# A decoder trunk on one core: feed-forward tiles in pairs, full-array compressed values, a second row by halves, another attention order

## The chip, the cores and the metric

The kernel runs on one core of a Trainium2 chip. TensorE (PE in the profile) multiplies: LDWEIGHTS brings a stationary operand of up to 128 x 128 into the array (PEld), MATMUL streams a moving operand of up to 512 columns past it and adds into PSUM. VectorE (DVE), ScalarE (ACT) and GpSimd (POOL) work element by element; ScalarE evaluates functions from a table, which ACT_TABLE_LOAD brings in. SyncE (SP) issues the DMAs. Each engine works through its own queue in order and waits for others by semaphores. The metric is the time of one execution on the device in microseconds; lower is better.

## The reference, cut to what matters

Two decoder layers over 256 tokens of 1024 values, in float32. Each has a half-step feed-forward in front and behind; the first layer mixes by a gated convolution, the second by sparse attention, whose keys and values are made once, from the state between the layers.

```python
def swiglu_ffn(x, w_in, w_out):
    gate, up = jnp.split(x @ w_in, 2, axis=-1)
    return (jax.nn.silu(gate) * up) @ w_out
...
v_c = compress(kv[:, :, 0, 1], pe_v, w1_v, w2_v)      # gelu(blocks @ w1) @ w2
...
for i in range(DEPTH):
    h = h + 0.5 * swiglu_ffn(rmsnorm(h, ffn1_norm[i]), ffn1_w_in[i], ffn1_w_out[i])
    hn = rmsnorm(h, mix_norm[i])
    h = h + (short_conv_mixer(hn, ...) if i < N_A_LAYERS else nsa_mixer(hn, ..., kv))
    h = h + 0.5 * swiglu_ffn(rmsnorm(h, ffn2_norm[i]), ffn2_w_in[i], ffn2_w_out[i])
```

A feed-forward goes from 1024 to 2 x 2816 and back. In attention each query takes three softmaxes: over 15 compressed blocks, over selected blocks and over a window. The queries are normalised per head (a reciprocal square root), and gates (sigmoid) weigh the three.

## The kernel before, in words

**Products by halves.** Every float32 operand is cut into a high part (rounded to the format that TensorE takes at full rate, "fp32r") and a low part (the rest). A weight unit of 128 x 1024 thus becomes two tiles: "wh", cast by ScalarE (line 165, Stream.high), and "wl", the difference, by VectorE (line 182, Stream.low). An activation tile "xs" or "act" holds 256 high and 256 low columns side by side. A product is then a *wide* one, wh against all 512 columns (line 353), and a *narrow* one, wl against the 256 high columns (line 358), summed in PSUM; the wide product's two halves are added when PSUM is read.

**Weights.** One stream W carries all weights in the order of their use. DMAs bring 1 MB pieces into three staging tiles "ws". pump casts units ahead: at most NBUF = 6 units (three column tiles) beyond those freed; take hands units out, done frees them. A `weave` interleaves one pump with each step of an evacuation and, if asked to (rest), fills up to the limit at its end.

**Feed-forward.** ffn_in runs over NF = 22 column tiles of 128 gates and 128 ups. For each, a_group does two columns: 16 wide products (2 columns x 8 rows of 128), then 16 narrow ones, into one of two PSUM buffers "mm". Then `total` reads the buffer (ScalarE line 367, VectorE line 368), ffn_evac multiplies by the row norm (372), applies SiLU (ScalarE 384, VectorE 385) and cuts the result into halves (361, 362). A callback bg does other work behind given tiles. There are four feed-forwards. The first begins in first_tiles, where three column tiles are computed row by row as x and the weights arrive; their sums wait, and while they are worked off, one more every third tile, only two units are pumped per tile. out_proj (lines 467 and 469) does the way back: per output column 22 wide and 22 narrow products.

**First rows.** In first_tiles row 0 is done by halves: first the 256 high columns of x, then the low ones. For each later row both halves of x, then the weights of columns 0 and 1, are cut in turn: `highs` on ScalarE (line 510), `lows` on VectorE (507); then the products (513).

**Shared keys and values.** In the third feed-forward bg does the compression: c_hidden of the values behind tile 14 (W1AT), c_total and its GELU behind tile 15 (gelu: GpSimd 820 to 825 with a ScalarE tanh at 823), kc_norm with a square root behind 16 (841, 843), c_values behind 17 (855, 858), which multiplies in four half-array blocks.

**Attention.** The stage is an order written out by hand: ORDER is a list of words, each an operation with its indices, issued in that order to the engines' queues. The words that matter here: GT, GC, GA, GX, GE, GD gates; qs, qr, root, recip, qn queries of the first half (squares, sums, square root at line 938, reciprocal, scaling at 960); exp the preloading of the table "natural_log_exp_and_others" (line 1192); QT, QC the transposition of queries and its copy (971, 975); F one step of the projection of the second half's queries (988 to 990); SQ, RD, NW, QM their squares, sums, a reciprocal root from a logarithm and an exponential (948, 949) and scaling; S scores, M minima, E exponentials (1060), R, N normalisation (N on GpSimd, with the ending _d on VectorE); T, H transpositions; C, CH, CPC copies out of PSUM (on ScalarE, with _d on VectorE); V, U products with values; CP transposition of the compressed weights; WA, WD a unit's high and low part; WO pieces of the output projection. The PSUM buffers "a" are four; two are held by the second half's queries until QM_1.

Of the kernel before, what the change touches and what calls it, by code (L numbers as in the profile page):

```python
# [16 lines left out]
P = 128  # L17
# [32 lines left out]


ORDER = """
GT qs_0 F qs_1 qr_0 F F qr_1 GC root WA_0 exp recip qn_0 F qn_1 QT_0 QC_0 GA GX F GE S_0 GD WA_1 M_0_1 QT_1 M_0_0
E_0_1 F F F E_0_0 R_0_1 F WD_0 SQ_0 R_0_0 N_0_1 S_1 RD_0 QC_1 M_1_0 M_1_1 F F F E_1_0 F CM_0 N_0_0 E_1_1 S_2 F F CX_0
R_1_0 N_1_0_d CE_0 R_1_1 F T_0_1 M_2_1 E_2_1 SQ_1 CR_0 C_0_1 N_1_1 T_1_0 M_2_0 RD_1 CG_0 C_1_0 CI_0 T_0_0 NW H_0 R_2_1
C_0_0 S_3 QM_0 CL_0 QM_1 M_3_1 T_1_1 E_2_0 CP_0 M_3_0 CH_0 CPC_0 QT_2 QC_2 C_1_1 N_2_1 E_3_0 H_1 QT_3 R_2_0 T_2_1
CH_1_d S_4 QC_3 E_3_1 CM_1 N_2_0 V_0 C_2_1_d R_3_0 M_4_0 M_4_1 T_2_0 CX_1 U_0 U_1 H_2 N_3_0 O_0 P_0 R_3_1 CE_1 CR_1
C_2_0_d N_3_1 E_4_1 S_5 CG_1 V_1 T_3_1 CH_2 M_5_1 E_4_0 R_4_1 T_3_0 M_5_0 H_3 CH_3_d CI_1 CM_2 S_6 C_3_1_d N_4_1 E_5_1
O_1 T_4_1 CL_1 R_4_0 C_3_0_d R_5_1 CP_1 P_1 M_6_1 WA_2 CX_2 CE_2 CR_2 CPC_1_d V_3 E_6_1 V_2 C_4_1 N_4_0 T_4_0 M_6_0
C_4_0_d U_3 H_4 CG_2 E_5_0 CI_2 E_6_0 CH_4_d N_5_1 R_5_0 N_5_0_d U_2 S_7 CL_2 O_2 CP_2 CPC_2 V_4 O_3 U_4 O_4 WA_3  # L60
R_6_1 M_7_0 T_5_0 P_3 R_6_0 WA_4 P_2 N_6_1 P_4 E_7_0 WD_1 M_7_1 CM_3 T_5_1 N_6_0 WD_2 H_5 WO_0_a T_6_1 WO_1_a C_6_1
CX_3 R_7_0 WD_3 CE_3 T_6_0 N_7_0 C_5_0_d CH_5 E_7_1 CR_3 CG_3 CI_3 C_5_1 WO_2_a WO_3_a C_6_0_d R_7_1 T_7_0 N_7_1_d
T_7_1 U_5 C_7_0 C_7_1_d CL_3 CP_3 CPC_3 H_7 WD_4 H_6 WA_5 CH_6_d U_6 CH_7_d V_5 V_6 O_5 O_6 P_5 P_6 V_7 U_7 WD_5 O_7
WO_1_b WO_0_b P_7 WO_0_c WO_3_b WO_1_c WO_2_b WO_3_c WO_2_c
"""


# [1 line left out]
def trunk(ctx, tc, A, out):  # L69
# [132 lines left out]
                self.pump()  # L202

    W = Stream()
    W1AT = (11, 14)
    W.add(A["ffn1_w_in"][0])
    W.add(A["ffn1_w_out"][0])
    W.add(A["conv_w_in"])
# [193 lines left out]
    def ffn_in(xs, norm, R=None, bg=None, pre=None, sums=()):  # L402

        hid, sums = [], list(sums)
        box = [R]
        n0 = len(sums)

        def mid():
            if pre is not None:
                pre()  # L410
            box[0] = norm.rows()

        for f in range(n0, NF):
            o = bank2()
            a_group([o[:, 0], o[:, 1]], xs, mid if f == n0 and R is None else None, not n0)
            sums.append(total(o, 2))
            late = len(sums) > 1
            weave(ffn_evac(sums.pop(0), box[0], hid), not late)
            if late and (f - n0) % 3 == 2:
                list(ffn_evac(sums.pop(0), box[0], hid))  # L420
            if bg is not None:
                bg(f)
        return hid

    def out_evac(o, c, factor, norm, short=False):
# [72 lines left out]
    def first_tiles():  # L498

        o = [bank2(), bank2()]  # L500
        oo, o = o, [[x[:, u] for u in range(2)] for x in o] + [[bank(), bank()]]
        w = [[mk([P, 2, 4, P], t, NBUF, F32R) for t in ("wh", "wl")] for _ in range(6)]

        def lows(f, src, g):
            wh, wl = w[2 * f + g[0] // 4]
            ks = slice(g[0] % 4, g[-1] % 4 + 1)
            ve.tensor_tensor(out=wl[:, :, ks], in0=src, in1=wh[:, :, ks].bitcast(F32), op=ALU.subtract)  # L507

        def highs(f, src, g, copy=ac.copy):
            copy(w[2 * f + g[0] // 4][0][:, :, g[0] % 4:g[-1] % 4 + 1], src)  # L510

        def product(f, k, u, x, c=slice(0, 512)):
            pe.matmul(o[f][u][:, c], w[2 * f + k // 4][x][:, u, k % 4], xs[k][:, c], start=k == x == c.start == 0, stop=(k == 7 and x == 1))

        def products(f, g):
            for x in range(2):
                for u in range(2):
                    for k in g:
                        product(f, k, u, x, slice(0, (2 - x) * T))

        def third(ks):
            g = range(*ks)
            src = w2st[:, ks[0] * 2 * P:ks[1] * 2 * P].rearrange("p (k u m) -> p u k m", u=2, m=P)
            highs(2, src, g)
            lows(2, src, g)

        def more(k):
            t = sq[0].rearrange("p a t -> p (a t)")
            po.tensor_tensor(out=t, in0=t, in1=sq[k].rearrange("p a t -> p (a t)"), op=ALU.add)

        nm.high(0)
        highs(0, parts[0, (0,)], (0,), ve.tensor_copy)
        highs(1, parts[1, (0,)], (0,))
        nm.low(0)
        for f in range(2):
            lows(f, parts[f, (0,)], (0,))
        for c in (slice(0, T), slice(T, 512)):
            for f in range(2):
                for u in range(2):
                    product(f, 0, u, 0, c)  # L540
        for f in range(2):
            for u in range(2):
                product(f, 0, u, 1, slice(0, T))
        third(THIRD[1])
        square(0)
        products(2, (0,))
        for n, g in enumerate(GROUPS):
            if n == 0:
                continue
            for k in g:  # L550
                nm.tile(k, False)
            for f in range(2):
                highs(f, parts[f, g], g)
                lows(f, parts[f, g], g)
            for k in g:
                square(k)
            for f in range(2):
                products(f, g)
            if n in (2, 4):
                third(THIRD[n + 1])  # L560
            if n < 5:
                products(2, g)
            if g[-1] % 2 and g[-1] > 1:
                more(g[-1] // 2)
        po.tensor_tensor(out=nm.sq, in0=sq[0][:, 0], in1=sq[0][:, 1], op=ALU.add)
        W.units += [None] * 6
        W.take(6)
        W.done(6, False)
        W.high()
        sums = [total(x, 2) for x in oo]  # L570
        products(2, GROUPS[-1])
        W.pump(1)
        r = t2([P, 2, T])
        for u in range(2):
            ac.copy(r[:, u], o[2][u][:, T:])
        for u in range(2):
            ve.tensor_tensor(out=r[:, u], in0=o[2][u][:, :T], in1=r[:, u], op=ALU.add)
        sums.append(r)
        W.pump(1)
        q = act()  # L580
        split(nm.sq, q)
        W.pump(2)
        return sums, q
# [266 lines left out]
    def c_values(a):  # L850

        pc = bank([P, 2, 64])
        t = t1([P, 2, 64])
        a4 = t1([P, 4, 4, 16])
        po.tensor_copy(out=a4, in_=a.rearrange("p (g n) -> p g n", g=4)[:, :, None, :].to_broadcast([P, 4, 4, 16]))
        for g in range(4):
            z = slice(g % 2 * 64, g % 2 * 64 + 64)
            pe.matmul(pc[z, g // 2], a4[:, g].rearrange("p x n -> p (x n)"), w2[1], start=True, stop=True)
        for g2 in range(2):
            hi, lo = slice(g2 * 64, g2 * 64 + 32), slice(g2 * 64 + 32, g2 * 64 + 64)  # L860
            ac.copy(vc[hi, :, g2], pc[hi])
            ac.copy(t[lo].bitcast(F32R), pc[lo])
            ve.tensor_tensor(out=vc[lo, :, g2], in0=pc[lo], in1=t[lo], op=ALU.subtract)

    def bg(f):
# [3 lines left out]
        elif f == 1:  # L869
            r = inv_rms(kv["s"])  # L870
            for tt in range(2):
                v = kns[tt].rearrange("p (n d) -> p n d", d=64)
                po.tensor_tensor(out=v, in0=v, in1=r[:, tt * 8:tt * 8 + 8, None].to_broadcast([P, 8, 64]), op=ALU.mult)
        elif f in (2, 3, 4, 5):
            c_trans((f - 2) % 2, (f - 2) // 2)
        elif f in (6, 7):
            k_trans(f - 6)
        elif f == 8:
            po.tensor_tensor(out=both, in0=ident[:, :64], in1=ident[:, 64:], op=ALU.add)
            po.tensor_tensor(out=both48, in0=ident[:96, :48], in1=ident[:96, 48:96], op=ALU.add)  # L880
        elif f == 9:
            kv["rk"] = rh_split(0)
        elif f == W1AT[0]:
            kv["ak"] = c_hidden(kv["rk"])
        elif f == 12:
            kv["ak"] = c_total(kv["ak"])
            kv["rv"] = rh_split(1)
            W.limit = NBUF
        elif f == W1AT[1]:
            kv["av"] = c_hidden(kv["rv"])  # L890
            kv["kc"] = kc_second(kv["ak"])
        elif f == 15:
            kv["av"] = c_total(kv["av"])
        elif f == 16:
            kc_norm(*kv["kc"])
        elif f == 17:
            c_values(kv["av"])

# [426 lines left out]
```

## Time and profile before

| | us |
|---|---|
| median of three runs (968.42 to 969.76) | 969.49 |
| the profiled execution, whole | 967.74 |
| its span, from the first to the last instruction | 965.8 |
| TensorE busy in the span | 960.5 |
| VectorE, ScalarE, GpSimd busy | 733.4, 571.2, 133.6 |

The granted clock of TensorE is 1.00 throughout the span. The stages on TensorE: first rows and first feed-forward to 129, its way back to 190, convolution to 279, second feed-forward with its way back to 464, keys and values to 497, third feed-forward with its way back to 690, query projection and attention to 767, output projection to 778, fourth feed-forward to the end.

In a list of instructions a row gives start, duration, engine, line, operation, written and read tile, shapes and count of merged neighbours; TensorE's durations overlap, since matmuls are pipelined, so its pace is read from starts. In the chain's rows the pieces follow one another without overlap. In a table of stretches each engine has its busy time and number of instructions; the columns after are the granted clock, the DMAs' share and GB/s. In a list of waits stand the waiting instruction, what it waited for, the sum, how often, and the longest.

### The profile page before, as it was taken

How to read it: one execution, taken by the hardware profiler on the slowest of the kernel's cores; microseconds unless marked ns; L12 is line 12 of the kernel's file. 1: busy time of each engine (PE TensorE's matmuls, PEld its weight loads, DVE VectorE, ACT ScalarE, POOL GpSimd, SP SyncE). 2: the span in 40 equal slices, each digit the busy share in tenths (PEclk: the TensorE clock that was granted, in tenths of full speed). 3: DMA queues.
4: the chain of work that ended last, by engine and by line, in shares of the span. 5: the costliest groups of instructions: out<-in, count | busy, mean ns of one | idle time of the engine just before them, and what ended most of it. 6: DMA issues, size and time to landing. Idle time of an engine off the chain costs nothing.

```text
span 965.8 us, 14561 instructions
## 1 busy us (share of the span) xinstructions
PE 960.5 (99%) x5614; PEld 841.4 (87%) x5614; DVE 733.4 (76%) x1152; ACT 571.2 (59%) x972; POOL 133.6 (14%) x217
## 2 busy tenths in 40 slices
PE   9999999999999999999999999999999999999998
PEld 8888888888888888888888888888877888888888
DVE  7888876578898787766549988866579898878652
ACT  7666654455566665645556676754589676566530
POOL 2000000144520000000111013000138320000000
PEclk9999999999999999999999999999999999999999
DMA  8656655545546875555535566555510356555550
GB/s 307 211 182 218 210 183 182 201 165 204 182 172 225 234 234 175 194 198 181 211 131 175 175 223 248 183 178 191 205 46 2 131 196 238 177 184 207 181 191 22
DMA packets 28433, 177.61 MB, mean 184 GB/s; under 512 B 3099, under 2 KB 6555, under 8 KB 7756
## 3 DMA queue, kind: packets, MB, share of 16 engines
q1 hardware_dynamic: 28364, 176.69, 53.6%
q8 instruction: 44, 0.72, 0.3%
q14 instruction: 25, 0.20, 0.1%
HBM read 175.59 MB, written 1.08 MB: 183 GB/s over the span
## 4 chain that ended last, share of the span: by engine, by line
PE 98%; DVE 1%; ACT 1%; DMA 0%; issue 0%; SPq 0%
PE mm L353 36%; PE mm L358 19%; PE a L467 17%; PE a L469 9%; PE a L353 3%; PE a L358 2%; PE mm L1041 1%; PE a L692 1%; PE a L694 1%; PE a L693 1%; PE a L1118 1%; PE a L1086 1%; DMA base<-in_first_dram 0%; DVE wl L507 0%; PE a L988 0%; PE a L801 0%
## 5 line engine op out<-in xcount | busy, mean ns | idle before, releaser
L182 DVE TENSOR_TENSOR wl<-ws,wh 128x1024 fp32r<-128x1024 f32 x318 | 392.3, 1248 | 97.5 <-PE a L469 63.0
L353 PE MATMUL mm<-xs,wh 128*128 128x512 f32 x1488 | 357.4, 392 | 0.0
L165 ACT CAST wh<-ws 128x1024 fp32r<-128x1024 f32 x318 | 328.2, 1046 | 38.5 <-PE a L467 20.5
L353 PEld LDWEIGHTS mm<-xs,wh 128*128 128x128 f32 x1488 | 273.1, 188 | 52.7
L358 PEld LDWEIGHTS mm<-xs,wl 128*128 128x128 f32 x1488 | 191.6, 191 | 7.8
L358 PE MATMUL mm<-xs,wl 128*128 128x256 f32 x1488 | 194.0, 283 | 0.0
L467 PE MATMUL a<-act,wh 128*128 128x512 f32 x714 | 169.1, 390 | 0.0
L467 PEld LDWEIGHTS a<-act,wh 128*128 128x128 f32 x714 | 131.8, 188 | 26.1
L368 DVE TENSOR_TENSOR t<-mm,t 128x512 f32<-128x512 f32 x95 | 65.4, 688 | 66.1 <-ACT t L367 65.3
L367 ACT COPY t<-mm 128x512 f32<-128x512 f32 x95 | 55.6, 585 | 89.6 <-PE mm L358 84.8
L469 PEld LDWEIGHTS a<-act,wl 128*128 128x128 f32 x714 | 90.6, 191 | 2.7
L469 PE MATMUL a<-act,wl 128*128 128x256 f32 x714 | 91.8, 283 | 0.0
L314 POOL TENSOR_TENSOR sq<-sq,t 128x256 f32<-128x256 f32 x35 | 27.7, 792 | 398.0 <-ACT t L312 397.9
L384 ACT ACTIVATE t<-t 128x256 f32<-128x256 f32 x88 | 36.9, 420 | 65.5 <-DVE t L372 65.4
L297 ACT ACTIVATE xs<-base 128x256 fp32r<-128x256 f32 x48 | 24.1, 505 | 77.6 <-DVE base L427 70.2
L372 DVE TENSOR_TENSOR t<-t,R 128x512 f32<-128x512 f32 x88 | 61.6, 700 | 2.6
L361 ACT CAST act<-t 128x256 fp32r<-128x256 f32 x96 | 39.0, 406 | 29.6 <-DVE t L621 19.4
L362 DVE TENSOR_TENSOR act<-t,act 128x256 fp32r<-128x256 f32 x96 | 41.0, 427 | 5.2 <-ACT act L361 5.2
L385 DVE TENSOR_TENSOR t<-t,t 128x256 f32<-128x256 f32 x88 | 36.9, 419 | 3.6 <-ACT t L384 3.5
L427 DVE SCALAR_TENSOR_TENSOR base<-a,base 128x256 f32<-128x256 f32 x78 | 32.8, 421 | 8.1 <-PE a L469 6.1
L301 DVE SCALAR_TENSOR_TENSOR xs<-base,xs 128x256 fp32r<-128x256 f32 x48 | 25.3, 529 | 11.0 <-ACT xs L297 10.9
L1060 ACT ACTIVATE pr<-pr,sm 128x128 f32<-128x128 f32 (+1 forms) x64 | 28.3, 448 | 1.9 <-DVE sm L1049 1.9
(261 smaller groups left out, 786.2 us busy)
## 6 DMA issues: line engine op xcount, KB each, us to landing
ws<-in_ffn_w_in_dram SPq DMA_DIRECT2D x85, 1024.0 KB, 4.9
ws<-in_ffn_w_out_dram SPq DMA_DIRECT2D x44, 1024.0 KB, 4.8
ws<-in_conv_w_in_dram SPq DMA_DIRECT2D x12, 1024.0 KB, 4.8
ws<-in_w_kv_dram SPq DMA_DIRECT2D x6, 1024.0 KB, 4.8
ws<-in_conv_w_out_dram SPq DMA_DIRECT2D x4, 1024.0 KB, 4.9
ws<-in_attn_w_q_dram SPq DMA_DIRECT2D x4, 1024.0 KB, 4.9
ws<-in_attn_w_o_dram SPq DMA_DIRECT2D x4, 1024.0 KB, 4.9
base<-row_d SPq DMA_DIRECT2D x8, 256.0 KB, 6.0
```

The source lines that it names most:

```text
L165: ac.copy(h, src)
L182: ve.tensor_tensor(out=l, in0=src, in1=h.bitcast(F32), op=ALU.subtract)
L353: pe.matmul(o, u[0][:, k * P:(k + 1) * P], xs[k], start=(k == 0), stop=False)
L358: pe.matmul(o[:, :T], u[1][:, k * P:(k + 1) * P], xs[k][:, :T], start=False, stop=(k == last))
L361: ac.copy(dst[:, :T], src)
L362: ve.tensor_tensor(out=dst[:, T:], in0=src, in1=dst[:, :T].bitcast(F32), op=ALU.subtract)
L367: ac.copy(r, o[:, :, T:])
L368: ve.tensor_tensor(out=r, in0=o[:, :, :T], in1=r, op=ALU.add)
L372: ve.tensor_tensor(out=r, in0=r, in1=R[:, None, :].to_broadcast([P, n, T]), op=ALU.mult)
L384: ac.activation(s, r[:, 0], AF.Silu)
L467: pe.matmul(o, run[k][0], lhs[k], start=(k == 0), stop=False)
L469: pe.matmul(o[:, :T], run[k][1], lhs[k][:, :T], start=False, stop=(k == n - 1))
```

## The change

Five edits. (1) ffn_in takes tiles in pairs: 16 wide products of the first tile, the second tile's two wide products of row 0, the first tile's 16 narrow, its evacuation and background work, the second tile's 16 narrow, its other 14 wide, its evacuation. The next pair's wide products follow directly. A tile with the norm's sum inside, and an odd last one, stay as they were. (2) c_hidden of the values moves from tile 14 to tile 15, with its weights in the stream, and c_total from 15 to 16, behind kc_norm. (3) c_values multiplies in two full-array products. (4) Row 1 in first_tiles is done by halves like row 0, with one weight cast on VectorE, and the third tile's products between. (5) ORDER is another permutation of the steps. In it C_3_0, C_3_1, CH_3, C_5_0, C_6_0, CH_6, CH_7 lose their _d, CPC_2 gains one, and N changes engine in six places.

```diff
 ORDER = """
-GT qs_0 F qs_1 qr_0 F F qr_1 GC root WA_0 exp recip qn_0 F qn_1 QT_0 QC_0 GA GX F GE S_0 GD WA_1 M_0_1 QT_1 M_0_0
-E_0_1 F F F E_0_0 R_0_1 F WD_0 SQ_0 R_0_0 N_0_1 S_1 RD_0 QC_1 M_1_0 M_1_1 F F F E_1_0 F CM_0 N_0_0 E_1_1 S_2 F F CX_0
-R_1_0 N_1_0_d CE_0 R_1_1 F T_0_1 M_2_1 E_2_1 SQ_1 CR_0 C_0_1 N_1_1 T_1_0 M_2_0 RD_1 CG_0 C_1_0 CI_0 T_0_0 NW H_0 R_2_1
-C_0_0 S_3 QM_0 CL_0 QM_1 M_3_1 T_1_1 E_2_0 CP_0 M_3_0 CH_0 CPC_0 QT_2 QC_2 C_1_1 N_2_1 E_3_0 H_1 QT_3 R_2_0 T_2_1
...
+qs_0 GT qr_0 qs_1 exp GC F qr_1 F root F F WA_0 recip qn_0 qn_1 QT_0 GA GX QC_0 F S_0 WA_1 WD_0 M_0_1 GE QT_1 M_0_0
+E_0_1 E_0_0 QC_1 F F R_0_1 F S_1 F F F GD M_1_1 M_1_0 N_0_1 R_0_0 F S_2 CM_0 F F F F E_1_1 R_1_1 CX_0 N_0_0_d SQ_0
+N_1_1 E_1_0 R_1_0 M_2_1 CE_0 N_1_0 T_0_1 T_0_0 E_2_1 SQ_1 C_0_1 C_0_0 RD_0 CR_0 M_2_0 RD_1 CG_0 CI_0 NW T_1_0 R_2_1
+QM_0 H_0 CH_0 S_3 E_2_0 QM_1 T_1_1 CL_0 M_3_0 M_3_1 QT_2 H_1 C_1_0 N_2_1 C_1_1 CP_0 CM_1 QC_2 T_2_1 CPC_0 R_2_0 E_3_1
...
-    W1AT = (11, 14)
+    W1AT = (11, 15)
...
-        for f in range(n0, NF):
-            o = bank2()
-            a_group([o[:, 0], o[:, 1]], xs, mid if f == n0 and R is None else None, not n0)
+        def finish(f, o):
             sums.append(total(o, 2))
             late = len(sums) > 1
             weave(ffn_evac(sums.pop(0), box[0], hid), not late)
...
+        def wide(o, us, ks, last=8):
+            for x in range(2):
+                for k in ks:
+                    pe.matmul(o[:, x], us[x][0][:, k * P:(k + 1) * P], xs[k], start=(k == 0), stop=(k == last))
+
+        def narrow(o, us, last=8):
+            for x in range(2):
+                for k in range(8):
+                    pe.matmul(o[:, x, :T], us[x][1][:, k * P:(k + 1) * P], xs[k][:, :T], start=False, stop=(k == last))
+
+        f = n0
+        while f < NF:
+            o = bank2()
+            if f == n0 and R is None or f + 1 == NF:
+                a_group([o[:, 0], o[:, 1]], xs, mid if f == n0 and R is None else None, not n0)
+                finish(f, o)
+                f += 1
+                continue
+
+            u = W.take(2)
+            wide(o, u, range(8))
+            o2, u2 = bank2(), W.take(2)
+            wide(o2, u2, [0])
+            narrow(o, u, 7)
+            W.done(2, False)
+            finish(f, o)
+            narrow(o2, u2)
+            wide(o2, u2, range(1, 8), 7)
+            W.done(2, False)
+            finish(f + 1, o2)
+            f += 2
...
+        def by_halves(k, mid):
+            nm.high(k)
+            highs(0, parts[0, (k,)], (k,), ve.tensor_copy)
+            highs(1, parts[1, (k,)], (k,))
+            nm.low(k)
+            for f in range(2):
+                lows(f, parts[f, (k,)], (k,))
+            for c in (slice(0, T), slice(T, 512)):
+                for f in range(2):
+                    for u in range(2):
+                        product(f, k, u, 0, c)
+            mid()
...
+        by_halves(0, lambda: None)
         third(THIRD[1])
         square(0)
         products(2, (0,))
+        by_halves(1, lambda: products(2, (1,)))
+        square(1)
...
-        for g in range(4):
-            z = slice(g % 2 * 64, g % 2 * 64 + 64)
-            pe.matmul(pc[z, g // 2], a4[:, g].rearrange("p x n -> p (x n)"), w2[1], start=True, stop=True)
+        for q in range(2):
+            pe.matmul(pc[:, q], a4[:, 2 * q:2 * q + 2].rearrange("p g x n -> p (g x n)"), w2[1], start=True, stop=True)
...
-        elif f == 15:
-            kv["av"] = c_total(kv["av"])
         elif f == 16:
             kc_norm(*kv["kc"])
+            kv["av"] = c_total(kv["av"])
```

More of the change, by code (lines that the diff above doesn't have):

```diff
@@ L52 @@
 ORDER = """
-GT qs_0 F qs_1 qr_0 F F qr_1 GC root WA_0 exp recip qn_0 F qn_1 QT_0 QC_0 GA GX F GE S_0 GD WA_1 M_0_1 QT_1 M_0_0
-E_0_1 F F F E_0_0 R_0_1 F WD_0 SQ_0 R_0_0 N_0_1 S_1 RD_0 QC_1 M_1_0 M_1_1 F F F E_1_0 F CM_0 N_0_0 E_1_1 S_2 F F CX_0
-R_1_0 N_1_0_d CE_0 R_1_1 F T_0_1 M_2_1 E_2_1 SQ_1 CR_0 C_0_1 N_1_1 T_1_0 M_2_0 RD_1 CG_0 C_1_0 CI_0 T_0_0 NW H_0 R_2_1
-C_0_0 S_3 QM_0 CL_0 QM_1 M_3_1 T_1_1 E_2_0 CP_0 M_3_0 CH_0 CPC_0 QT_2 QC_2 C_1_1 N_2_1 E_3_0 H_1 QT_3 R_2_0 T_2_1
-CH_1_d S_4 QC_3 E_3_1 CM_1 N_2_0 V_0 C_2_1_d R_3_0 M_4_0 M_4_1 T_2_0 CX_1 U_0 U_1 H_2 N_3_0 O_0 P_0 R_3_1 CE_1 CR_1
@@ L58 @@
[L58 to L62, printed above, removed]
@@ L63 @@
-T_7_1 U_5 C_7_0 C_7_1_d CL_3 CP_3 CPC_3 H_7 WD_4 H_6 WA_5 CH_6_d U_6 CH_7_d V_5 V_6 O_5 O_6 P_5 P_6 V_7 U_7 WD_5 O_7
-WO_1_b WO_0_b P_7 WO_0_c WO_3_b WO_1_c WO_2_b WO_3_c WO_2_c
+qs_0 GT qr_0 qs_1 exp GC F qr_1 F root F F WA_0 recip qn_0 qn_1 QT_0 GA GX QC_0 F S_0 WA_1 WD_0 M_0_1 GE QT_1 M_0_0
+E_0_1 E_0_0 QC_1 F F R_0_1 F S_1 F F F GD M_1_1 M_1_0 N_0_1 R_0_0 F S_2 CM_0 F F F F E_1_1 R_1_1 CX_0 N_0_0_d SQ_0
+N_1_1 E_1_0 R_1_0 M_2_1 CE_0 N_1_0 T_0_1 T_0_0 E_2_1 SQ_1 C_0_1 C_0_0 RD_0 CR_0 M_2_0 RD_1 CG_0 CI_0 NW T_1_0 R_2_1
@@ new lines @@
+QM_0 H_0 CH_0 S_3 E_2_0 QM_1 T_1_1 CL_0 M_3_0 M_3_1 QT_2 H_1 C_1_0 N_2_1 C_1_1 CP_0 CM_1 QC_2 T_2_1 CPC_0 R_2_0 E_3_1
+QT_3 N_2_0 S_4 CH_1_d QC_3 C_2_1_d R_3_1 V_0 T_2_0 CX_1 E_3_0 H_2 M_4_0 U_0 CE_1 E_4_0 M_4_1 CH_2 C_2_0_d R_3_0 U_1
+O_0 N_3_1 E_4_1 CR_1 S_5 CG_1 V_1 CI_1 M_5_0 M_5_1 O_1 R_4_0 R_4_1 V_2 S_6 T_3_1 N_3_0 CM_2 P_0 T_3_0 E_5_1 P_1 CL_1
+CX_2 CE_2 N_4_1_d H_3 C_3_1 C_3_0 CR_2 CH_3 R_5_1 N_4_0 T_4_1 C_4_1 CG_2 CP_1 M_6_1 CI_2 CPC_1_d CL_2 T_4_0 E_5_0 V_3
+C_4_0_d H_4 U_2 M_6_0 O_2 U_3 CH_4_d R_5_0 WD_1 E_6_0 CP_2 O_3 CPC_2_d N_5_1 S_7 R_6_0 E_6_1 N_5_0 V_4 U_4 P_3 P_2
@@ L65 @@
+N_6_0 O_4 M_7_0 T_5_1 E_7_0 T_5_0 P_4 M_7_1 WA_2 H_5 R_6_1 CM_3 WO_0_a N_6_1_d WD_2 CX_3 T_6_0 C_5_1 CH_5 CE_3 WO_1_a
+E_7_1 T_6_1 CR_3 H_6 CG_3 C_6_1 R_7_0 CI_3 N_7_0_d C_6_0 CL_3 WO_2_a CP_3 U_5 CH_6 R_7_1 C_5_0 N_7_1_d CPC_3 T_7_0
+C_7_0 T_7_1 WA_3 H_7 WD_3 U_6 V_5 WA_4 CH_7 O_5 V_6 C_7_1_d V_7 O_6 U_7 P_6 P_5 WO_0_b O_7 WD_4 WO_2_b P_7 WO_0_c
+WO_1_b WO_3_a WO_1_c WO_3_b WA_5 WD_5 WO_3_c WO_2_c
 """
@@ L529, in more @@
             po.tensor_tensor(out=t, in0=t, in1=sq[k].rearrange("p a t -> p (a t)"), op=ALU.add)
[L531 to L537, printed above, removed]
+        def by_halves(k, mid):
[10 more added lines that the diff above has]
+            mid()
             for f in range(2):
                 for u in range(2):
[L540 to L543, printed above, removed]
+                    product(f, k, u, 1, slice(0, T))
+        by_halves(0, lambda: None)
         third(THIRD[1])
@@ L546, in first_tiles @@
         products(2, (0,))
+        by_halves(1, lambda: products(2, (1,)))
+        square(1)
         for n, g in enumerate(GROUPS):
-            if n == 0:
+            if n < 2:
                 continue
```

## The prediction

> **What bounds the kernel now.** I read the page first, then TensorE's waits, then the chain that ended last.
>
> ```profile
> PE 960.5 (99%) x5614; PEld 841.4 (87%) x5614; DVE 733.4 (76%) x1152; ACT 571.2 (59%) x972; POOL 133.6 (14%) x217
> ```
>
> ```profile
> PE mm L513 <- ACT wh L510: 0.8, 1, 0.8
> PE a L1086 <- ACT xs L1096: 0.4, 1, 0.4
> ```
>
> ```profile
> 28.91 3.65 PE mm L353 x16
> 32.57 1.91 PE mm L358 x16
> ...
> 117.98 3.65 PE mm L353 x16
> ...
> 144.45 5.01 PE a L467 x22
> 149.46 2.63 PE a L469 x22
> ```
>
> TensorE is busy for 99% of the span and past its warm-up waits twice, for 0.8 and 0.4 us. So the kernel gets faster only by shorter TensorE work, and every wait put into TensorE's queue is paid in full. The third fence shows what there is to shorten. A column tile is 16 wide and 16 narrow products, and from 28.91 to 117.98 lie 16 tiles: 5.567 us each. A column of an output projection, 22 and 22, takes 5.01 + 2.63 = 7.64. The six further pairs cost 2.07 us, 0.346 a pair; 16 pairs are 5.54, which leaves about 0.02 us a tile for the turn from narrow to wide and back. That is all that touching can save.
>
> **The change part by part.** *Pairs.* Numbering a phase's tiles from 0, the first feed-forward has pairs (4,5) to (20,21), the second and fourth (1,2) to (19,20), the third (0,1) to (20,21): 9 + 10 + 10 + 11 = 40, each one turn fewer. In seven pairs of the third the background's own products stand between the groups, so I count 33: 33 x 0.02 = **-0.6** (0 to -0.8).
>
> Against that stand three terms. In a pair the second tile starts its k = 0 wide products right behind the first tile's 16 wide ones, 3.65 us after the pair's start, where before it began 5.57 after; its second column at 3.88. By then its high weights must be cast, and the PSUM buffer of the tile before the pair (there are two) must be read out.
>
> ```profile
> 28.75 0.63 PE L353 MATMUL mm<-xs,wh 128*128 128x512 f32 x2
> ```
>
> ```profile
> 32.12 1.03 ACT L165 CAST wh<-ws 128x1024 fp32r<-128x1024 f32 x1
> ```
>
> ```profile
> 62.15 0.40 PE L353 MATMUL mm<-xs,wh 128*128 128x512 f32 x1
> ```
>
> ```profile
> 65.81 1.04 ACT L165 CAST wh<-ws 128x1024 fp32r<-128x1024 f32 x1
> ```
>
> *High weights, first feed-forward.* Up to tile 11, while three early sums are worked off, only two weight units are made per tile (weave without its rest), so a tile's weights come one tile ahead. Tile 4 starts at 28.75. Tile 5's second cast ends at 33.15, 4.40 after, and is wanted at 3.88: with 0.06 for the signal a wait of 0.6. Tile 10 starts at 62.15; tile 11's second cast ends at 66.85, 4.70 after, late because the extra evacuation after tile 8 fills VectorE. In a pair tile 9 ends 5.1 us behind tile 8, not 5.57, so add 0.5: wanted at 3.88, there at 5.2, a wait of 1.3. The pairs between have nothing extra ahead of them. Sum **+1.9** (1.0 to 2.0). What is late behind it is nothing: later casts run three tiles ahead.
>
> ```profile
> 784.24 3.80 PE L353 MATMUL mm<-xs,wh 128*128 128x512 f32 x16
> ```
>
> ```profile
> 788.55 0.62 DVE L368 TENSOR_TENSOR t<-mm,t 128x512 f32<-128x512 f32 x1
> ```
>
> ```profile
> 532.52 3.90 PE L353 MATMUL mm<-xs,wh 128*128 128x512 f32 x16
> ```
>
> ```profile
> 536.26 0.69 DVE L368 TENSOR_TENSOR t<-mm,t 128x512 f32<-128x512 f32 x1
> ```
>
> ```profile
> 285.94 3.35 PE L353 MATMUL mm<-xs,wh 128*128 128x512 f32 x14
> ```
>
> ```profile
> 289.15 0.62 DVE L368 TENSOR_TENSOR t<-mm,t 128x512 f32<-128x512 f32 x1
> ```
>
> *Buffers.* In the fourth feed-forward tile 1 starts at 784.24, tile 2 wants tile 0's buffer at 787.89, and VectorE, which had weight conversions and the reciprocal in front, has read it at 789.17: 1.3. In the third, tile 6 starts at 532.52 behind transpositions (0.1 more until it is wanted: 536.26), and tile 5's buffer is read at 536.95: 0.7. In the second, wanted at 289.59, read at 289.77: 0.2. Sum **+2.2** (0.5 to 2.4; the fourth's lag hangs on how the attention stage hands over).
>
> ```profile
> 593.70 0.56 PE L812 MATMUL a<-both,t 128*128 128x64 f32 x4
> ```
>
> ```profile
> 598.63 0.40 ACT L361 CAST act<-t 128x256 fp32r<-128x256 f32 x1
> 598.93 0.20 ACT L814 COPY t<-a 128x64 f32<-128x64 f32 x1
> ```
>
> ```profile
> 602.02 0.40 POOL L855 COPY t<-t 128x256 f32<-128x256 f32 x1
> ```
>
> ```profile
> 605.07 1.28 ACT L843 ACT_TABLE_LOAD   x1
> 606.37 0.31 ACT L843 ACTIVATE t<-a,epst 128x64 f32<-128x64 f32 x1
> ```
>
> ```profile
> 605.62 0.45 PE L858 MATMUL a<-small,t 128*64 128x64 f32 x8
> ```
>
> *Compressed values.* Two full-array products for four half-array ones: the group at 605.62 costs 0.39 us to the next product and a turn of some 0.1; the four full instructions at 593.70 take 0.37, so **-0.1** (0 to -0.2). What moves is dearer. Before, c_total stands behind tile 15 (593.70). ScalarE gets to its copy only after the tile's own evacuation, at 598.93; GELU and the spreading copy end at 602.42, and c_values at 605.62 finds them done. In the changed kernel c_total stands behind tile 16's narrow products, after kc_norm, and c_values behind tile 17. Since 16 and 17 are a pair, only tile 17's narrow products (1.91), 14 wide ones (3.2) and 0.5 for the two small groups lie between: 5.6 us. The chain is longer. ScalarE's queue for the tile lasts to 599.03, 5.3 after the tile's end, some of it a backlog; I take 4.6 (4.0 to 5.3). Then kc_norm's table load and square root, 1.6, now in front of the copy; then 3.5 from copy to spread values. 9.7 against 5.6: **+4.1** (3.5 to 4.8). Behind the blocked matmul all of TensorE waits.
>
> *Second row by halves.*
>
> ```profile
> 7.08 0.69 ACT L510 CAST wh<-base 128x256 fp32r<-128x256 f32 x2
> ```
>
> Row 1's first products wait for the first of two ScalarE casts (the 0.8 above, to 7.83). One cast goes to VectorE, idle there, and the first half needs no low part of x, so TensorE can start at about 7.3. The row was 0.55 late, and its gain is bounded by that; later rows hang on ScalarE and VectorE, from which one cast of 0.3 is gone: **-0.3** (0 to -0.55).
>
> *Attention order.* The same 258 steps. On TensorE I find the same products and about two fewer turns into score or half-column blocks: nothing to speak of. But "exp", the preloading of the exponential table, now stands before "root", the stage's square root.
>
> ```profile
> 703.41 0.22 ACT L938 ACTIVATE sm<-sm 128x18 f32<-128x18 f32 x1
> ```
>
> ```profile
> 703.96 1.29 DVE L960 TENSOR_TENSOR t<-mm,sm 128x512 f32<-128x512 f32 x2
> ```
>
> ```profile
> 705.58 0.60 PE L971 MATMUL a<-small,t 128*128 128x128 f32 x4
> ```
>
> ```profile
> 722.39 0.24 ACT L948 ACTIVATE sm<-sm 128x16 f32<-128x16 f32 x1
> ```
>
> ```profile
> 725.36 0.60 PE L971 MATMUL a<-small,t 128*128 128x128 f32 x4
> ```
>
> ```profile
> 701.00:706.00 5.00, 5.00 (x25) 3.94 (x24) 3.43 (x8) 3.84 (x6) 0.22 (x1) 1.00 0.63 210
> 706.00:712.00 6.00, 6.00 (x37) 4.47 (x35) 4.26 (x23) 4.84 (x17) 0.40 (x1) 1.00 0.02 4
> 712.00:718.00 6.00, 6.00 (x38) 4.31 (x36) 5.29 (x28) 5.62 (x23) 5.07 (x11) 1.00 0.01 1
> 718.00:724.00 6.00, 5.62 (x39) 4.44 (x37) 5.08 (x30) 5.35 (x20) 3.38 (x10) 1.00 0.01 1
> 724.00:730.00 6.00, 5.97 (x50) 4.35 (x50) 5.68 (x32) 6.00 (x22) 4.39 (x11) 1.00 0.00 0
> ```
>
> After the preload the square root needs its own table again (as at L843, 1.28 each), and the next exponential another. If that one is the plain exponential table, the logarithm of "NW" and the exponential behind it need one each as well: four loads more, 5.1 us of ScalarE. First place: preload and load sit between qs_1 and root, where ScalarE has at most 1.16 idle (5.00 - 3.84); I let them fill 0.75 of it, so root comes 1.8 late; the normalised queries, done at 705.25 before, come at 707.1, and QT_0, at 705.58 before, waits 1.5. Second: NW's logarithm, at 722.39 before, comes about 1.5 late (idle slices of ScalarE absorb part of the load before the gates) and brings two loads; QT_2, 725.36 before, hangs on it through VectorE and comes 4.0 late, with CP_0 (0.4), which stood before it, still to do. From 724 on ScalarE is busy 6.00 of 6.00 and TensorE 5.97, so the lag stays: **+4.4**. Ends: 1.8, if all 3.35 us idle up to 724 swallow loads; 6.5, if none does and the copies that lose their "_d" (to ScalarE, net six) add to it.
>
> The Trainium skill, page "ScalarE: Activation LUTs", section "Table sets: the hidden batching unit", states that exponential then square root means two loads since they are in different sets, and that logarithm and exponential share one named set, which speaks against this order. It prices a switch at about 2.66 us with a drain. By 2.66 the four would be 10.6 and the time some 5.5 us longer; the row at 605.07 shows the square root 1.30 after the load's start, no drain. On the sets the trace agrees: NW's logarithm and exponential run without a load between them.
>
> **The sum**: -0.6 - 0.1 - 0.3 + 1.9 + 2.2 + 4.1 + 4.4 = **+11.6 us**. The profiled execution took 967.74, so 979.3; the median of the three runs is 1.75 above it, and I predict by the median: 969.49 + 11.6 = **981.1**.
>
> **The rivals.**
> - *Loads not repeated*: the compiler keeps a table that serves, or the preload takes effect only at the first exponential. Then the 4.4 goes, 976.7. For it: no row shows a preload overwritten. Against: every square root in the trace that follows another function has its load. 0.12.
> - *Values covered*: ScalarE and GpSimd reach tile 16's small copy early, and the 4.1 goes: 977.0. Against: ScalarE's queue is in order, and the copy stands behind the tile's own casts. 0.06.
> - *Drains*: the skill's price holds, 986.6. 0.03.
> - *Faster, by pace*: wide products that touch run quicker than 0.227. A pair has 32, 40 pairs 1,280; the waits of 12.6 less the other gains 1.0 are met at 9 ns each, so it decides from a pace below 218 ns; at 216 the time is 967. Against: 22 wide in a row already touch, and their six further ones cost 5.01 - 3.65 = 1.36, 0.227 each, as in a run of 16. 0.05.
> - *Nothing to measure*: the waits shrink to what the gains pay, since each wait lets ScalarE and VectorE catch up for the next: 969.5. Against: the two large ones are first of their kind in stages 100 us apart. 0.04.
>
> **How the numbers follow.** The forecast has 0.70. The bounds of the terms added up give 974.7 to 985.2, a little more with the 1.3 by which the runs of before spread, and the two rivals without one large term fall inside; outside are pace, nothing and drains (0.12) and the forecast's tails (0.06). Range 974.0 to 986.0. About 0.2% (2 us) can be told from no change. Faster 0.05; same 0.04; slower 0.91.
>
> **What would show it.** Right: a wait of L858 on GpSimd of 3 to 5 us; of L971 on VectorE of about 1.5 after the first queries; four or more table loads between 700 and 730 instead of one; waits of L353 on ScalarE at tiles 5 and 11 and on VectorE at tile 2 of the fourth feed-forward; pairs of 11.11 us where none waits. Wrong: one table load in the attention stage, or no wait at L858; a pair much under 11.1 would bring the pace.

## The result, and the profile after

| | before | after |
|---|---|---|
| median, us (six runs each) | 969.11 (968.42 to 969.76) | 980.54 (978.40 to 981.84) |
| the profiled execution, us | 967.74 | 978.47 |
| its span, us | 965.8 | 976.6 |

The ratio is 1.0115, with a 95% interval from 1.0100 to 1.0131: the changed kernel is slower by 11.4 us, against 11.6 forecast. The profiled executions differ by 10.7. The page of the changed kernel, first its line of engines:

```profile
PE 962.8 (99%) x5614; PEld 841.5 (86%) x5614; DVE 731.6 (75%) x1157; ACT 580.1 (59%) x982; POOL 127.0 (13%) x207
```

TensorE has the same 5614 products and is 99% busy as before, but its idle time, the span less the busy time, grew from 5.3 to 13.8 us; the other 2.3 of the 10.8 are listed as busy. Its waits show where (waiting instruction, releaser, sum, times, longest):

```profile
PE a L893 <- POOL t L891: 2.7, 1, 2.7
PE mm L425 <- DVE t L368: 1.7, 2, 1.2
PE a L1005 <- DVE t L994: 1.6, 4, 0.9
PE a L1120 <- ACT act L1130: 1.6, 1, 1.6
PE mm L425 <- ACT wh L165: 1.6, 2, 1.1
PE a L253 <- DVE ones L228: 1.1, 1, 1.1
PE a L1120 <- ACT xs L1130: 0.4, 1, 0.4
```

The last two were there before (a third, of 0.8 at row 1, is gone); the first five are new, 9.2 us. L425 is the pair's wide product, L893 c_values, L1005 the transposition of queries, L1120 the transposition T of the probabilities. By stages, from the starts of TensorE's rows in both traces:

| stage on TensorE | before | after | difference | forecast |
|---|---|---|---|---|
| first product of row 0 to tile 3 | 18.44 | 17.80 | -0.64 | -0.3 |
| tile 3 to the first way back | 106.03 | 108.26 | +2.24 | +1.7 |
| convolution's way back to the second feed-forward's | 134.54 | 134.71 | +0.17 | 0.0 |
| third feed-forward | 130.94 | 134.76 | +3.82 | +4.6 |
| query projection to the output projection's last piece | 77.28 | 81.36 | +4.08 | +4.4 |
| fourth feed-forward | 122.97 | 124.17 | +1.20 | +1.1 |
| sum | | | +10.87 | +11.5 |

The forecast's column is its terms with the turns saved in each stage taken off. What lies between these stages differs by 0.02 us at most.

One thing was not in the forecast. Of the six runs three show a granted clock of 1.000 (978.40, 978.47, 979.71) and three one of 0.996 to 0.998 (981.37, 981.68, 981.84). Of the 72 runs of the kernel before in the experiments 70 show 1.000 and two 0.999. So the median lies 12.1 above 968.47, the median of those 72, and the profile, taken at 1.000, only 10.7 above its like.

### The profile page after: what moved, and what is told of

Same layout as the page of the kernel before. It is cut to its first block, busy times and chain, and to the rows that moved or that the text cites. A ratio compares the mean times of both kernels' runs of the same rounds, so it can differ in the third digit from the quotient of the medians.

```text
span 976.6 us, 14569 instructions
## 1 busy us (share of the span) xinstructions
PE 962.8 (99%) x5614; PEld 841.5 (86%) x5614; DVE 731.6 (75%) x1157; ACT 580.1 (59%) x982; POOL 127.0 (13%) x207
## 4 chain that ended last, share of the span: by engine, by line
PE 88%; DVE 8%; ACT 3%; issue 1%; POOL 0%; ACTq 0%; POOLq 0%; DVEq 0%
PE mm L425 26%; PE a L497 16%; PE mm L430 14%; PE a L499 8%; PE mm L353 5%; DVE wl L182 3%; PE mm L358 2%; PE a L353 2%; PE mm L543 1%; PE mm L1075 1%; PE a L728 1%; PE a L730 1%; PE a L729 1%; PE a L358 1%; ACT wh L165 1%
## 5 line engine op out<-in xcount | busy, mean ns | idle before, releaser
L425 PE MATMUL mm<-xs,wh 128*128 128x512 f32 x1280 | 302.0, 391 | 3.4 <-DVE t L368 1.7
L425 PEld LDWEIGHTS mm<-xs,wh 128*128 128x128 f32 x1280 | 236.6, 188 | 53.0 <-DVE t L368 3.9
L430 PEld LDWEIGHTS mm<-xs,wl 128*128 128x128 f32 x1280 | 159.1, 191 | 3.1
L430 PE MATMUL mm<-xs,wl 128*128 128x256 f32 x1280 | 161.0, 283 | 0.0
L353 PE MATMUL mm<-xs,wh 128*128 128x512 f32 x208 | 51.0, 393 | 0.0
```

The source lines that it names most:

```text
L353: pe.matmul(o, u[0][:, k * P:(k + 1) * P], xs[k], start=(k == 0), stop=False)
L425: pe.matmul(o[:, x], us[x][0][:, k * P:(k + 1) * P], xs[k], start=(k == 0), stop=(k == last))
L430: pe.matmul(o[:, x, :T], us[x][1][:, k * P:(k + 1) * P], xs[k][:, :T], start=False, stop=(k == last))
```

## The experiments

In this section a number for a kernel is its median over 4 to 11 runs, beside runs of the kernel before on the same chip.

**1. "exp" behind root.**

```diff
-qs_0 GT qr_0 qs_1 exp GC F qr_1 F root F F WA_0 recip ...
+qs_0 GT qr_0 qs_1 GC F qr_1 F root F F WA_0 exp recip ...
```

> The changed kernel with one word moved: exp, the preloading of the table, stands behind WA_0 again, so behind root. Theory (table loads): one load between 700 and 735 instead of five; the waits of QT_0 and QT_2 go; from the gates' first product to the output projection's last piece 66.0 us (65.5 to 66.5) instead of 69.97, as in the kernel before; the time about 4 us below the changed kernel's, 976.5. Rival (the order itself, its copies moved to ScalarE): the stage stays within 1 us of 70 and the time within 1 us of 980.5.

The profiled run, with a clock of 1.000, took 974.84: 3.6 under the changed kernel's. The attention stage went from 81.36 to 77.22 us (77.28 before), and of TensorE's new waits those of L1005 and L1120 are gone. So all of the +4.08 is the one word, and the order around it is worth nothing either way. First ScalarE's list in the changed kernel, then TensorE's (start, duration, instruction, and in brackets the idle time before it and what ended it):

```profile
707.83 1.28 ACT L1226 ACT_TABLE_LOAD   x1
...
709.51 1.28 ACT L972 ACT_TABLE_LOAD   x1
710.80 0.22 ACT L972 ACTIVATE sm<-sm 128x18 f32<-128x18 f32 x1
...
714.92 1.28 ACT L1053 ACT_TABLE_LOAD   x1
...
729.69 1.28 ACT L982 ACT_TABLE_LOAD   x1
730.98 0.22 ACT L982 ACTIVATE sm<-sm 128x16 f32<-128x16 f32 x1
731.22 1.28 ACT L983 ACT_TABLE_LOAD   x1
732.51 0.22 ACT L983 ACTIVATE sm<-sm 128x16 f32<-128x16 f32 x1
732.63 0.57 ACT L1130 COPY act<-a 128x512 f32<-128x512 f32 x1
```

```profile
730.02 1.65 PE L1075 MATMUL mm<-kt,act 64*128 64x288 f32 x12
733.25 0.66 PE L1120 MATMUL a<-small,pr 128*128 128x128 f32 x4 [1.59 <-ACT act L1130]
734.14 0.33 PE L1005 MATMUL a<-small,t 128*128 128x128 f32 x1 [0.23 <-DVE t L994]
```

The preload (L1226) brings the table with logarithm and exponential and nothing uses it: root (L972) loads another. From there each function gets a table that holds it but not the next: the gates' exponential (L1053), NW's logarithm (L982), its exponential (L983). Behind the last stands the copy that T_1_1 needs its PSUM buffer from, and TensorE waits 1.59 us. With exp behind root the list has a single load in this stretch:

```profile
710.45 1.28 ACT L1226 ACT_TABLE_LOAD   x1
```

The other runs, at 0.997 to 0.998, took 977.18 to 978.31. So the median, 977.74, missed its 976.5: the drop of the clock doesn't need the table loads.

**2. exp ahead of root in the kernel before.** The same word, alone, in the old order.

```diff
-GT qs_0 F qs_1 qr_0 F F qr_1 GC root WA_0 exp recip ...
+GT qs_0 F qs_1 exp qr_0 F F qr_1 GC root WA_0 recip ...
```

> The kernel before with one word moved: exp stands behind qs_1, ahead of root; nothing else. Theory (table loads): five loads in the attention stage instead of one; the stage 4 us longer (3 to 5): 973. Rival (a load costs only where it is followed by a matmul that waits; in the old order ScalarE has room): under 1 us, 969 to 970.

973.39 against 968.65 (ratio 1.0054, 1.0042 to 1.0067), the stage 82.27 instead of 77.28. ScalarE's list:

```profile
702.92 1.28 ACT L1192 ACT_TABLE_LOAD   x1
...
704.60 1.28 ACT L938 ACT_TABLE_LOAD   x1
...
709.08 1.28 ACT L1019 ACT_TABLE_LOAD   x1
...
725.55 1.28 ACT L948 ACT_TABLE_LOAD   x1
...
727.08 1.28 ACT L949 ACT_TABLE_LOAD   x1
```

Again five loads. 5.0 us for the four that are more, 5.1 us of ScalarE: nothing hides them in the old order. One of its five runs has a clock of 0.998, 2.2 us above the highest of the others.

**3. c_values one tile later.**

```diff
-        elif f == 17:
+        elif f == 18:
             c_values(kv["av"])
```

> The changed kernel with c_values behind tile 18 instead of 17. Theory (values wait): the 2.7 us wait of line 893 on GpSimd is gone and nothing takes its place; the third feed-forward is 3.0 us shorter; runs at a granted clock of 1.000: 975.5. Clock theory (the idle TensorE there makes the gate drop in some runs): besides, no run of this kernel shows a granted clock under 1.000 and its runs no longer fall in two groups 3 us apart, so the median falls by 3 to 6. Rival for the two groups (the stage of the table loads, or the chip): some runs still show 0.998.

The wait is gone, and the third feed-forward takes 131.70 instead of 134.76: -3.06, as expected. The median was 976.87, not 975.5, since two of the four runs were still at 0.998 (the one at 1.000 took 975.93): the rival for the two groups held. The stretches of the profiled run, at 0.998, show where (PE, PEld, DVE, ACT, POOL busy; behind them the granted clock):

```profile
725.30:728.70 3.40, 3.02 (x27) 2.43 (x25) 1.41 (x8) 3.35 (x7) 1.21 (x4) 1.00 0.00 0
728.70:732.10 3.40, 1.36 (x9) 0.56 (x5) 1.86 (x7) 3.39 (x10) 1.09 (x4) 0.99 0.00 0
732.10:735.50 3.40, 3.36 (x16) 3.37 (x17) 3.32 (x21) 2.52 (x7) 1.47 (x4) 0.50 0.00 0
735.50:738.90 3.40, 3.40 (x33) 2.36 (x31) 2.02 (x11) 3.40 (x16) 3.32 (x9) 1.00 0.02 5
```

For 3.4 us TensorE ran at half its clock, right behind the two loads of NW, where it had worked 1.36 of 3.40 us. The attention stage took 82.75 instead of 81.36.

**4. A longer wait at c_values.** Ten more spreading copies on GpSimd ahead of the products.

```diff
         a4 = t1([P, 4, 4, 16])
+        for _ in range(10):
+            po.tensor_copy(out=a4, in_=a.rearrange("p (g n) -> p g n", g=4)[:, :, None, :].to_broadcast([P, 4, 4, 16]))
```

> The changed kernel with ten more spreading copies (0.4 us each on GpSimd) ahead of c_values' products: the wait of line 893 becomes about 4 us longer, some 7 us. Clock theory: a wait that fills a whole window halves the clock in every run: granted clock 0.998 or less in all of them, no two groups, and a time of about 980.5 + 4 + 1.5 to 3, so 986 to 988 (the fast group's 978.4 + 4 + 3 = 985.5 at the least). Rival (clock has nothing to do with this wait): 978.4 + 4 in about half of the runs with a clock of 1.000 (982.5), 985.5 in the others.

989.33, and all four runs have a clock of 0.993 to 0.995. The wait grew by 7.0 us, not 4 (the copies took 0.7 each), so the time is above the expected 988; the third feed-forward grew by 9.89, which leaves 2.85 for the clock. Stretches of this kernel:

```profile
600.00:606.00 6.00, 6.00 (x46) 5.76 (x45) 5.66 (x7) 4.57 (x9) 0.00 (x0) 1.00 0.82 280
606.00:612.00 6.00, 2.96 (x13) 2.08 (x12) 4.34 (x9) 5.76 (x9) 2.11 (x7) 0.94 0.81 300
612.00:618.00 6.00, 0.00 (x0) 0.00 (x0) 4.12 (x5) 2.94 (x4) 5.51 (x9) 0.50 0.15 25
618.00:624.00 6.00, 5.27 (x14) 4.33 (x15) 0.58 (x2) 1.02 (x4) 0.61 (x2) 0.50 0.37 152
624.00:630.00 6.00, 6.00 (x41) 5.52 (x40) 0.95 (x2) 1.54 (x2) 0.00 (x0) 0.93 0.00 0
```

The clock falls inside the wait and comes back 6 us after TensorE resumed at 618.73. So a wait that is long enough costs its own length and some 3 us more. That the changed kernel's 2.7 us sometimes does so too is inferred: in experiment 1 it is the only wait over 1.2 us that is left, and three of the four runs lost clock; no trace was taken of such a run.

**5. Both repairs together.**

> The changed kernel with both repairs that were run singly: exp behind root, c_values behind tile 18. What stays are the waits of the pairs, the longest 1.3 us. Theory (clock): the two places where the clock dropped in some runs, the values' wait and the table loads' waits, are gone, so every run has a granted clock of 1.000 and the runs lie within 1.5 us of each other. Theory (sum): 978.47 - 4.14 (query projection's start to output projection's end, 81.36 to 77.22) - 3.06 (third feed-forward, 134.76 to 131.70) = 971.3. Rival (other waits drop the clock too): some runs at 0.999 or less and 2 us above the others.

Five runs from 971.54 to 973.15, all at 1.000; the stages 131.69 and 77.22 as expected. The median, 972.45, is 1.1 above the sum, which the start may account for: the profiled run's start to tile 3 took 19.78 us, where the sum used a profile with 17.80. Either place alone leaves runs that lose clock, and with both gone none of five does; so the pairs' waits of up to 1.2 us don't drop it.

**6. The third feed-forward unpaired**, its values left at their new places. In this and the next kernels p0 is the first tile that may begin a pair; here p0 = NF in the third.

```diff
-            if f == n0 and R is None or f + 1 == NF:
+            if f < p0 or f == n0 and R is None or f + 1 == NF:
```

> The changed kernel, with the third feed-forward's tiles one by one again; its values stay at their new places (c_hidden behind 15, c_total behind 16 and kc_norm, c_values behind 17). Theory (the wait comes from the values being a tile later; pairing shortens the time between only from 5.57 to 5.1): the wait of line 893 on GpSimd stays at 2.2 to 2.5 us, tile 7's wait of 0.7 goes, the third feed-forward is 1.0 to 1.3 us shorter than the changed kernel's 134.76, and about half of the runs still show a granted clock under 1.000. Rival (pairing makes the wait): the wait under 0.5 and the stage 3 us shorter or more, clock 1.000.

```profile
PE a L893 <- POOL t L891: 2.3, 1, 2.3
```

The wait stays at 2.3 us, and the stage is 133.35, 1.41 shorter (a little more than expected). Three of the four runs have a clock of 0.998, where about half were expected; the fourth, the profiled one, has 0.999, and its clock falls only at 975.0, behind TensorE's last products. So the wait comes from the places to which the values moved, and the pairing itself adds 0.4 to it. The places have two parts that no run separates: one tile less between c_total and c_values, and kc_norm in front of c_total's copy, which takes 1.5 us by ScalarE's list further below.

**7. The second row by halves, alone**, in the kernel before.

> The kernel before with the second row by halves and nothing else. The traces of before and after show the fourth column tile starting 0.64 us earlier, more than the 0.55 that the prediction took as its bound. Theory (the halves bring it): that start at 22.3 instead of 22.92 and the time 0.6 below the kernel before. Rival (scatter of the weights' arrival between two profiles): within 0.2 of it, in start and time.

Tile 3 started at 22.91, as before, and the median of eleven runs, 968.00, is 0.5 under 968.49 (ratio 0.9996, 0.9987 to 1.0005): not to be told from nothing. From row 0's first product to tile 3 the profiles give 18.44, 19.05 and 19.49 us without the halves, and 17.49 to 19.78 with them. The -0.64 of the table above lies within that scatter, and no gain can be read from it.

**8. Pairs only where weights and buffers are there.** The kernel before with the halves and full-array values; pairs from tile 12 in the first feed-forward, from 3 in the second and fourth, none in the third. First with the order of before, then with the changed one and exp behind root.

```diff
-    hid = ffn_in(xs, First(), sums=sums)
+    hid = ffn_in(xs, First(), sums=sums, p0=12)
...
-    hid = ffn_in(xs, nm, pre=lambda: list(tab), bg=bias_bg)
+    hid = ffn_in(xs, nm, pre=lambda: list(tab), bg=bias_bg, p0=3)
...
-    hid = ffn_in(xs, None, R1, bg)
+    hid = ffn_in(xs, None, R1, bg, p0=NF)
...
-    hid = ffn_in(xs, nm)
+    hid = ffn_in(xs, nm, p0=3)
```

> The kernel before with the halves and the full-array values, in the attention order of before, and pairs only where weights and buffers are there: first feed-forward from tile 12, second and fourth from tile 3, third none (its values at their places of before). Theory (the changed kernel's losses are its waits, and touching saves a turn a pair): none of the waits at lines 425 and 893; 5 + 9 + 9 = 23 pairs x 0.02 = 0.46, halves 0.6, values 0.1, so 1.2 us under the kernel before, granted clock 1.000 throughout. Rival (a pair costs something besides its waits, by its evacuations coming in twos): within 0.5 of the kernel before or above it.

> The kernel of the run before this one, with the changed kernel's attention order but exp behind root. Theory (the order is worth nothing without the loads; the stage took 65.82 us in the run with exp behind root, 65.88 before): within 0.3 us of the run before this one. Rival (its copies moved to ScalarE and its other sequence cost or bring something once the stage starts on time): over 0.5 us either way.

968.18 and 968.08 against 968.49 (ratios 0.9998, 0.9989 to 1.0007, and 0.9994, 0.9985 to 1.0002): the 1.2 us did not come. The two are alike, as expected: the order is worth nothing. All large waits are gone, and by stages the second feed-forward is 0.18 shorter (nine turns) and the third 0.11 (the values), but the first is 0.18 and the fourth 0.18 longer. TensorE's list of the first of the two has the reason:

```profile
81.32 7.70 PE L425 MATMUL mm<-xs,wh 128*128 128x512 f32 x32
88.86 4.00 PE L430 MATMUL mm<-xs,wl 128*128 128x256 f32 x32
92.70 7.44 PE L425 MATMUL mm<-xs,wh 128*128 128x512 f32 x32
99.98 4.00 PE L430 MATMUL mm<-xs,wl 128*128 128x256 f32 x32
103.81 7.44 PE L425 MATMUL mm<-xs,wh 128*128 128x512 f32 x32
```

From 92.70 to 103.81 a pair takes 11.11 us, two tiles of 5.567 less 0.02: the turn is what the forecast said. The run of wide products at 81.32 took 0.26 longer than the next (7.54 to the narrow ones, against 7.28): two small waits ahead of tile 15. The fourth feed-forward has the like at tile 4, 0.24 and 0.11.

**9. Pairs a little later**: the last kernel with p0 = 16 and 5 for 12 and 3.

> The kernel of the run same_new_order with the pairs of the first feed-forward from tile 16 instead of 12 and of the fourth from tile 5 instead of 3. Theory (the small waits that were left, 0.15 and 0.11 at tile 15, 0.24 and 0.11 at tile 4, come from evacuations that are still behind): they go; first feed-forward 105.97 (3 pairs, 0.06 below the kernel before), fourth 122.81 (8 pairs, 0.16 below), so 0.5 us under that run and 0.8 to 0.9 under the kernel before. Rival (every first pair of a phase waits, wherever it stands): waits of 0.2 to 0.3 at the new first pairs and no gain on that run.

967.20 against 968.89: 0.9985 (0.9976 to 0.9994). The first feed-forward took 105.99, the fourth 122.73, without a wait at L425. Once more, beside the same kernel without the halves:

> The kernel of the run pairs_from_16_3_5 with the first rows of before, so without the second row by halves. The fourth tile's start scatters from 22.3 to 24.3 us over the profiles so far, in kernels with and without the halves, so profiles can't settle the halves; medians of many runs on one chip may. Theory (the halves save about what the prediction said, 0.3): 0.2 to 0.6 above the next kernel of this call, and 0.4 to 0.8 under the kernel before. Rival (they save nothing): equal to the next kernel within 0.2.

> The kernel of the run pairs_from_16_3_5 again, beside the one without the halves. Theory: 0.8 to 1.5 us under the kernel before, as the run before showed 1.5 and the profile's stages 0.6 behind the fourth tile's start. Rival (that run was a lucky draw): within 0.5 of the kernel before.

967.34 with and 967.43 without, against 968.25 (ratios 0.9991, 0.9982 to 1.0000, and 0.9992, 0.9983 to 1.0001). So this version lies some 0.9 to 1.7 us under the kernel before, at the edge of what can be told. By stages 0.6 is accounted for: 0.04 in the first feed-forward, 0.18 in the second, 0.11 in the third, 0.03 in attention, 0.24 in the fourth. The halves can't be seen in the pair of runs.

## Why the prediction was right, and where it was off

*What bounds it.* Right: every new wait was paid in full, and somewhat more; a pair saves 0.02 us. (The prediction's own figures, 5.567 less 5.54, give 0.03; the 0.02 that it used is what the pairs show.) The rival "pace" fell: 32 wide products that touch, from 92.70 to 99.98 in the last list, take 0.2275 each.

*High weights, first feed-forward.* Right in place and size at tiles 5 and 11. TensorE's list of the changed kernel:

```profile
32.57 0.50 PE L425 MATMUL mm<-xs,wh 128*128 128x512 f32 x1 [0.41 <-ACT wh L165]
...
67.34 0.50 PE L425 MATMUL mm<-xs,wh 128*128 128x512 f32 x1 [1.15 <-ACT wh L165]
```

The bracket holds only the idle time; from start to start the gaps are 0.80 and 1.55 against 0.23 for a product that doesn't wait, so 0.6 and 1.3, as forecast. "What is late behind it is nothing" was wrong: the products just behind a wait run slower too (at tile 4 and 5, 18 wide took 4.80 us to the narrow ones, 4.11 where none waits, so 0.69 for that 0.57), and a third wait, at tile 15, cost 0.3. Hence +2.24 for +1.7.

*Buffers.* Right: 1.35 at tile 2 of the fourth, 0.68 at tile 7 of the third, 0.24 in the second; forecast 1.3, 0.7, 0.2.

*Compressed values.* Right in mechanism, off in size. ScalarE's list, and the end of GpSimd's, in the changed kernel:

```profile
606.16 0.41 ACT L361 CAST act<-t 128x256 fp32r<-128x256 f32 x1
606.59 1.28 ACT L879 ACT_TABLE_LOAD   x1
607.88 0.31 ACT L879 ACTIVATE t<-a,epst 128x64 f32<-128x64 f32 x1
608.10 0.20 ACT L850 COPY t<-a 128x64 f32<-128x64 f32 x1
608.32 1.28 ACT L859 ACT_TABLE_LOAD   x1
609.61 0.26 ACT L859 ACTIVATE t<-t 128x64 f32<-128x64 f32 x1
```

```profile
610.66 0.40 POOL L891 COPY t<-t 128x256 f32<-128x256 f32 x1
```

c_total's products start at 602.59. ScalarE's queue for the tile lasts to 606.57, 4.0 after (I took 4.6, from a range of 4.0 to 5.3: the tile taken as the model had a backlog that this one had not); the square root and its table take 1.5 (1.6); from copy to spread values 608.10 to 611.06, 3.0 (3.5). 8.5 for 9.7, against 5.5 that lie between: 3.0 where I had 4.1, and the run with c_values a tile later gave 3.06. The wait itself, 2.7, lies under the 3 to 5 named as its sign. The 0.1 for the full-array products came out at 0.11.

*Attention.* Right: four loads more, between root and NW, +4.08 for +4.4. At the first place TensorE's list has waits of 0.93 and 0.20 at QT_0, 1.1 for 1.5. The second place was off by one instruction: not QT_2 but T_1_1 ahead of it took the wait, behind a copy that ScalarE had queued after NW's loads. The rival "loads not repeated" fell. So did "drains": L972 runs 1.29 after the start of its load, L983 1.29. Four loads more cost the stage 4.08 here and 4.99 in experiment 2, so 1.0 to 1.25 each. The price that the Trainium skill names, page "ScalarE: Activation LUTs", section "What ACT_TABLE_LOAD costs", about 2.66 us a switch, is not what these loads cost.

*Second row by halves.* -0.3 is neither shown nor refuted: the medians came out 0.5 lower in experiment 7 and 0.1 in experiment 9, neither clear of noise (the interval of the first reaches from -1.3 to +0.5).

*What the sum left out.* The clock. The terms came to 11.6, the profiled run, at a clock of 1.000, to 10.7. Half of the runs lost about 3 us more, by experiments 1, 3 and 5 at c_values or behind NW's loads: against 968.47 the three at 1.000 have a median 10.0 above, the three others 13.2, and the median of all six falls between the groups. That the forecast met it to 0.6 us is in part luck: two terms were too large (compressed values, attention), one too small (high weights), and one was missing. The row to read was there: a single wait of 4 us, in a kernel whose TensorE had none over 0.8, should have raised the question whether the clock would hold.

## What to carry to other kernels

Where one engine is busy for 99% of the span, a reordering that makes operands wanted earlier has to be priced by how far ahead each of them is made; here 0.02 us a pair was bought with waits of 0.2 to 1.3, and starting the pairs where evacuations and casts had caught up took the loss away and left, at most, a gain at the edge of what can be told. A preload of a function table belongs behind the last function of another table; one word ahead of a square root cost four loads and 4 to 5 us. And a wait of 2 to 3 us on TensorE can be dearer than its length, since the clock may fall behind it.

## What the runs showed of the hardware

A half clock came behind waits that were not whole stretches of idleness. In the run of experiment 3 TensorE had worked 1.36 of the 3.40 us ahead of the drop; whether a run drops varies from execution to execution of one program, as the three and three of the changed kernel show. The drop lasted 3.4 us there (732.1 to 735.5) and 13.7 in experiment 4 (by finer stretches 611.2 to 624.9), four times as long. The Trainium skill, page "TensorE: Matmul & The Clock Gate", section "Part 1: The HAM clock gate (the "warmup" mystery)", has a free-running window of 3413 ns and a half clock after at least one idle window. On the length and on the chance the trace agrees; on the idle window it differs, by that 1.36 us of work. How little work is enough was not tried on purpose, but the fourteen traces bear on it.

In all of them the clock's changes lie whole multiples of 3.41 us apart. Counted in steps of that length from the clock's first change, the clock fell behind every step at full clock in which TensorE was busy for 1.44 us or less, the steps at the kernel's end included, and behind none with 1.56 or more. (The profile models where a product ends, so the busy times are rough.) Two steps with the wait of c_values, the first in experiment 4's kernel, where the clock fell at 611.24, the second in experiment 1's, where it held:

```profile
607.83:611.24 3.41, 1.13 (x5) 0.58 (x4) 1.80 (x6) 3.37 (x7) 1.42 (x5) 1.00 0.69 221
```

```profile
607.15:610.56 3.41, 1.56 (x7) 0.94 (x6) 1.95 (x5) 3.37 (x6) 1.10 (x4) 1.00 0.66 202
```

In the changed kernel's trace the wait of 2.7 us lies across two steps, which keep 1.78 and 2.31 us of work, and the clock held. So whether such a wait drops the clock would hang on where the steps begin in that execution; no trace of a run that dropped behind this wait shows it.
